# More gathers in the gates' stage, weight subtractions on GpSimd in four pieces, and w_ple's products behind the queries

## The chip, the cores and the metric

One core of a Trainium2 chip runs the whole kernel in one launch. The metric is device time in microseconds; the time of a kernel is the median of its runs. Engines are named as in the profile: PE (TensorE matmuls), PEld (its weight loads), DVE (VectorE), ACT (ScalarE), POOL (GpSimd), SP (SyncE, which here only issues DMAs).

## The reference

One layer of an encoder on 512 tokens of width 1024, in fp32. Cut to what matters here:

```python
h = rms_norm(x, norm_mix); proj = h @ w_in            # q, k, v of two attentions, two gates
merged = sigmoid(gate_na) * (out_na @ w_branch_na) + sigmoid(gate_dil) * (out_dil @ w_branch_dil)
x = x + merged @ w_out
h = rms_norm(x, norm_ffn); x = x + peer_ffn(h, ...)   # below
h = rms_norm(x, norm_ple)
x = x + sigmoid(h @ w_ple_gate) * (p @ w_ple)

# peer_ffn, 8 heads, 128 x 128 = 16384 experts of one neuron each:
q = h @ w_query                                       # per head two halves of 128
s1, s2 = q[..., :128] @ k1.T, q[..., 128:] @ k2.T
v1, i1 = top_k(s1, 16); v2, i2 = top_k(s2, 16)
sc, pos = top_k(v1[..., :, None] + v2[..., None, :], 16)
eidx = (i1 * 128 + i2) at pos;  g = softmax(sc)
a = u[eidx] . h;  act = gelu(a) * g;  out = sum act * v[eidx]
```

## The kernel before

Weights come through `Stream` W (L115 to L161): SP loads a raw block of 128 x 1024 (L130; three buffers), ACT casts it to its high half `wh` (L141), and DVE or POOL subtracts that from the raw block, which gives the low half `wl` (L142). Which of the two engines does it stands in the block's spec ("v" or "p", L122, L203). There are five pairs of halves; a product of two fp32 matrices is three matmuls, high x high, high x low and low x high (`mm3`, L163).

The experts are computed in two ways. For tokens 128 to 511 (three token blocks) the kernel is dense: it multiplies with all 128 blocks of 128 experts. `up(b)` (L1001) makes `aT` with 24 matmuls of 384 columns, ACT takes its gelu; the result is multiplied by a matrix G of gate weights; `down` (L1137) multiplies with the block's `v`, 18 matmuls of 512 columns, into six PSUM banks `outs`. For tokens 0 to 127 it gathers: `experts0` (L929) has 256 units, 128 of u and 128 of v; each is one indirect DMA on POOL of 128 rows of 4 KB into one of three buffers `gath` (L940, L941) and one DVE operation that reads it (L952 for u, L960 for v, which adds into `acc0`).

The order in the part around the change:

- merge and w_out (`xo`, L821 to L835), each token block followed by its norm (`norm_parts`, L741); behind the last of them `ple(0)` and `ple(1)` (L806, L836), p @ w_ple into a DRAM buffer, stored from ACT's queue.
- the queries (`qp`, L967) with scores and the top 16 on DVE (`top16`, L756).
- the gates' stage (L1056 to L1106): the 76 blocks "ahead" (`ahead`, L1028: `up` of blocks 0 to 75, stored to DRAM as `ge`) run beside the selection of the experts (`select_steps`, L868) and beside the building of G, 48 groups of one-hot products: DVE makes `o` (L1080) and `m` (L1085), PE multiplies them (`gp`, L1094), ACT copies them to `stage`.
- the down stage (L1154 on): per block `down`, and for the other 52 blocks also `up`; it reads `ge` and G back from DRAM. The order of fresh and stored blocks is written out in `order` (L1014 to L1024).
- the end: `done(exp_side)` (L1170), then for each of the four token blocks the third norm (`third`, L1184), whose transpositions `pt` go through PE, and the products with w_ple_gate (`pg`, L1202).

What runs "beside" is a `Side` (L41): each step of the main order reports its planned time to `tick` (L99), and each side advances by that time multiplied by its rate. For the gathers one unit costs 1.0; the rate is RATE_GATES in the gates' stage (L1058), zero while the rest of the blocks ahead is finished, RATE_HEAD for the first four blocks of the down stage, and then so set that what is left ends EARLY = 30 planned us ahead of the last block (L1157). `issue_after(latest[0])` keeps a unit behind the DVE operation marked last. The tile framework then puts each engine's queue in order, by its own simulated timeline, and sets the waits.

Of the kernel before, what the change touches and what calls it, by code (L numbers as in the profile page):

```python
# [10 lines left out]
F32 = mybir.dt.float32  # L11
# [22 lines left out]
NSP = 76  # L34

RATE_LAST, RATE_HEAD, AHEAD = 0.0, 0.1, 1.0
RATE_G, RATE_GATES, EARLY = 1.45, 0.15, 30.0
CPK = 8 + 2 + 2 + 32 + 128


# [24 lines left out]
def block_kernel(ctx: ExitStack, tc: tile.TileContext, a: dict):  # L65
    nc = tc.nc
# [14 lines left out]
    def bank(tag, name):  # L81
        return psum.tile([128, 512], F32, tag=tag, name=name, bufs=2)

    x2_d = dram.tile([3, 128, D], F32, name="x2_d")
    ple_d = dram.tile([S, D], F32, name="ple_d")
# [29 lines left out]
    class Stream:  # L115
# [17 lines left out]
        def pump(self, most=99):  # L133
            self.fetch()
            while most and len(self.cut) < len(self.raw) and len(self.cut) < self.freed + self.parts:
                i = len(self.cut)
                _, n, eng = self.specs[i]
                shape = [128, n, 1024 // n]
                hi = self.pool.tile(shape, F32R, tag=self.tag + "h", name=self.tag + "h", bufs=self.parts)
                lo = self.pool.tile(shape, F32R, tag=self.tag + "l", name=self.tag + "l", bufs=self.parts)  # L140
                nc.scalar.copy(hi, self.raw[i])  # L141
                (nc.vector if eng == "v" else nc.gpsimd).tensor_sub(lo, self.raw[i], hi.bitcast(F32))  # L142
                self.raw[i] = None
                self.cut.append((hi, lo))
                self.fetch()
                most -= 1
# [14 lines left out]
    W = Stream(wp, "w", 3, 5)  # L161

    def mm3(ps, st, mv, start, stop):  # L163
        nc.tensor.matmul(ps, st[0], mv[0], start=start, stop=False)  # L164
        nc.tensor.matmul(ps, st[0], mv[1], start=False, stop=False)  # L165
        nc.tensor.matmul(ps, st[1], mv[0], start=False, stop=stop)  # L166
# [33 lines left out]
    wpl = a["w_ple"][0].rearrange("(k p) c -> p k c", p=128)  # L200
    wpg = a["w_ple_gate"][0].rearrange("(k p) c -> p k c", p=128)

    def add_block(w, c0, width=512, lo="v"):  # L203
        n = 1024 // width
        for q in range(w.shape[1] // n):
            W.add(w[:, n * q:n * q + n, c0:c0 + width], n, lo[q % len(lo)])
# [12 lines left out]
    pT = a["pT"].rearrange("(k p) t -> p k t", p=128)  # L219
    for b in range(2):  # L220
        add_block(wo, 512 * b, lo="vp")
    for b in range(2):
        W.add(pT, 2)
        add_block(wpl, 512 * b)
    for b in range(4):
        add_block(wq, 512 * b, lo="p" if b else "vp")


    hhi = hpool.tile([128, 8, S], F32R, name="hhi")
# [71 lines left out]
    def cell(ps, st_of, units, last, mv_of=None):  # L301

        n = units[0][0].shape[1]
        nk = n * len(units)
        for u, (hi, lo) in enumerate(units):
            for k in range(n):
                kk = u * n + k
                w = (hi[:, k], lo[:, k])
                if mv_of is None:
                    mm3(ps, st_of(kk), w, kk == 0, kk == nk - 1)  # L310
                else:
                    mm3(ps, tuple(x[:, mv_of[0]] for x in w), st_of(kk), kk == 0, kk == nk - 1)
            if last:
                W.free()
            yield 3 * n * ps.shape[-1] / 2400
# [456 lines left out]
    x2p = x2s.enter_context(tc.tile_pool(name="x2p", bufs=1, side="right"))  # L772
# [6 lines left out]
    def run(gen):  # L779
        for dt in gen:  # L780
            tick(dt)

    for b in range(2):
        units = W.take(1)
        for c in range(4):
# [3 lines left out]
            ps = bank("Q", "p2")  # L789
            run(tcell(ps, units, c, (odil, odil[:, 2:4]), c == 3))  # L790
            nc.vector.tensor_mul(g, ps, g)
        units = W.take(2)
        for c in range(4):
# [4 lines left out]
            ps = bank("P", "p1")  # L798
# [4 lines left out]
            nc.vector.tensor_sub(hlo[:, cc], s, hhi[:, cc].bitcast(F32))  # L803


    def ple(b):  # L806
        (phi, plo), = W.take(1)
        units = W.take(1)
        for n in range(4):
            ps = bank("P", "pl")  # L810
            ts = slice(128 * n, 128 * n + 128)
            run(cell(ps, lambda k: (phi[:, k, ts], plo[:, k, ts]), units, False))
            po = x2p.tile([128, 512], F32, tag="po", name="po", bufs=2)
            nc.scalar.copy(po, ps)
            nc.scalar.dma_start(ple_d[128 * n:128 * n + 128, 512 * b:512 * b + 512], po)
        W.free()
        W.free()


    ss2 = x2p.tile([128, 4, 2], F32, name="ss2")  # L820
    for b in range(2):  # L821
        cols = slice(512 * b, 512 * b + 512)
        units = W.take(4)
        for n in range(4):
            ps = bank("A", "xo")
            ts = slice(128 * n, 128 * n + 128)
# [4 lines left out]
            if b:  # L831
# [1 line left out]
                    nc.scalar.dma_start(x2_d[n - 1], y)  # L833
                hn = x2p.tile([128, D], F32, tag="hn", name="hn", bufs=2) if n else h2n
                norm_parts(y, gffn, hn, ss2[:, n], ts)  # L835
    ple(0)  # L836
    ple(1)
    x2s.close()
    gts.close()
    at.close()  # L840
# [2 lines left out]
    gel = ctx.enter_context(tc.tile_pool(name="gel", bufs=1))  # L843
# [123 lines left out]
    for b in range(4):  # L967
        units = W.take(4)
        for c in range(4):
            ps = bank("A", "qp")  # L970
# [22 lines left out]
    tqs.close()  # L993


    for b in range(NB):
        W.add(a["uT"][b].rearrange("p (k e) -> p k e", k=8), 8)
    for b in range(2):
        add_block(wpg, 512 * b)

# [16 lines left out]
    k = 0  # L1017
# [41 lines left out]
    for n in range(3):  # L1059
# [13 lines left out]
        for q in range(NG):  # L1073
# [15 lines left out]
            for g in range(OG // BG):  # L1089
                gpb = bank("PC"[g % 2], "gp")  # L1090
                for x in range(BG):
                    cs = slice(128 * (BG * g + x), 128 * (BG * g + x) + 128)
# [61 lines left out]
    for i, (b, fresh) in enumerate(order):  # L1154
# [3 lines left out]
        ge = whole(b) if fresh else None  # L1158
# [7 lines left out]
    units = V.take(len(pend))  # L1166
# [29 lines left out]
    for b in range(2):  # L1196
        cols = slice(512 * b, 512 * b + 512)
        units = W.take(4)
        for n in (0, 1, 2, 3):
            ps = bank("A", "pg")  # L1200
            ts = slice(128 * n, 128 * n + 128)
            run(cell(ps, lambda k: (hhi[:, k, ts], hlo[:, k, ts]), units, n == 3))  # L1202
            pl = fin.tile([128, 512], F32, tag="pl", name="pl", bufs=2)
# [76 lines left out]
```

## Time and profile before

| | us |
|---|---|
| median of 3 runs | 1830.58 (1828.13 to 1830.72) |
| the profiled execution | 1832.46 |
| its span | 1830.7 |

| engine | busy us | share of the span |
|---|---|---|
| PE | 1776.4 | 97% |
| DVE | 1326.1 | 72% |
| ACT | 730.1 | 40% |
| POOL | 483.3 | 26% |

The span is the time from the first to the last instruction of the program in one execution; all positions below are microseconds from its start. A busy share is a mean over stages that have different limits, so the rows further down go by stage. "Idle before" an instruction is time in which its engine did nothing, and the releaser is what ended last of that for which it waited. The granted clock is a share of PE's full speed.

### The profile page before, as it was taken

The numbers are of one execution on the slowest core, as the hardware profiler recorded it, in microseconds if no ns is written. First come the engines' busy times: TensorE is split into PE (matmuls) and PEld (weight loads), VectorE is DVE, ScalarE is ACT, GpSimd is POOL, SyncE is SP. The second block draws the span as 40 slices with busy tenths as digits, with TensorE's granted clock in tenths as the row PEclk, the third lists the DMA queues.
The fourth block names the chain that finished last, engine by engine and source line by source line (L and its number), as shares of the span: only waits on it lengthen the run. The fifth ranks groups of instructions, "written<-read, shape, count | busy, mean of one in ns | idle before, by whom it ended". The sixth has DMA issues, their size and how long they took to land.

```text
span 1830.7 us, 26023 instructions
## 1 busy us (share of the span) xinstructions
PE 1776.4 (97%) x9613; PEld 1563.2 (85%) x9613; DVE 1326.1 (72%) x2642; ACT 730.1 (40%) x1195; POOL 483.3 (26%) x328
## 2 busy tenths in 40 slices
PE   8999999999999999999999999999999999999938
PEld 7997777788788999999999888888888888888827
DVE  6634644436658999988885778888888788786864
ACT  5434553442433545444444333333334233333312
POOL 4201111111233011121210334344334344343320
PEclk9999999999999999999999999999999999999969
DMA  5231123333422475777778799899999999899842
GB/s 189 74 92 45 48 55 116 90 118 124 168 97 93 148 245 174 268 289 268 277 276 315 270 358 333 320 346 360 354 326 334 362 329 341 302 345 345 305 136 81
DMA packets 158383, 417.10 MB, mean 228 GB/s; under 512 B 14000, under 2 KB 59312, under 8 KB 155184
## 3 DMA queue, kind: packets, MB, share of 16 engines
q1 hardware_dynamic: 119808, 277.54, 43.7%
q0 software_dynamic: 36864, 134.23, 20.6%
q10 hardware_dynamic: 1584, 3.67, 0.5%
q8 instruction: 75, 1.23, 0.3%
q14 instruction: 52, 0.43, 0.1%
HBM read 368.73 MB, written 45.88 MB: 226 GB/s over the span
## 4 chain that ended last, share of the span: by engine, by line
PE 54%; issue 19%; DMA 15%; POOL 5%; DVE 5%; ACT 1%; SPq 0%; POOLq 0%; DVEq 0%; ACTq 0%
PE out L1144 9%; DMA gath<-peer_expert_v,eidx 6%; POOL gath L941 5%; PE aT L165 4%; PE aT L164 4%; PE aT L166 4%; PE proj L164 3%; PE proj L165 3%; DMA gr<-ge_d 3%; PE proj L166 3%; DMA gath<-peer_expert_u,eidx 3%; DMA vr<-peer_expert_v 2%; PE gt L164 2%; PE gt L165 2%; PE gt L166 2%
## 5 line engine op out<-in xcount | busy, mean ns | idle before, releaser
L165 PE MATMUL aT<-hlo,wh 128*128 128x384 f32 x1024 | 345.1, 337 | 0.0
L166 PE MATMUL aT<-hhi,wl 128*128 128x384 f32 x1024 | 344.7, 337 | 0.0
L164 PE MATMUL aT<-hhi,wh 128*128 128x384 f32 x1024 | 344.7, 337 | 0.0
L141 ACT CAST wh<-wr 128x1024 fp32r<-128x1024 f32 x216 | 226.7, 1051 | 272.5 <-PE aT L165 214.5
L941 POOL DMA_INDIRECT gath<-peer_expert_u,eidx x128 | 191.0, 1493 | 540.0 <-DVE gath L952 376.3
L142 DVE TENSOR_TENSOR wl<-wr,wh 128x1024 fp32r<-128x1024 f32 x188 | 237.2, 1263 | 112.6 <-ACT wh L141 111.7
L941 POOL DMA_INDIRECT gath<-peer_expert_v,eidx x128 | 169.7, 1326 | 281.2 <-DVE acc L960 212.5
L1144 PE MATMUL out<-vh,ahi 128*128 128x512 f32 x768 | 235.0, 393 | 5.4 <-ACT ahi L1132 5.4
L1144 PE MATMUL out<-vl,ahi 128*128 128x512 f32 x768 | 239.3, 391 | 0.4 <-DVE vl L142 0.4
L1144 PE MATMUL out<-vh,alo 128*128 128x512 f32 x768 | 235.8, 392 | 0.0
L141 ACT CAST vh<-vr 128x1024 fp32r<-128x1024 f32 x128 | 134.2, 1050 | 158.3 <-DMA vr<-peer_expert_v 90.6
L165 PEld LDWEIGHTS aT<-hlo,wh 128*128 128x128 f32 x1024 | 192.4, 188 | 2.6
L164 PEld LDWEIGHTS aT<-hhi,wh 128*128 128x128 f32 x1024 | 192.5, 188 | 2.5
L960 DVE SCALAR_TENSOR_TENSOR acc<-gath,act,acc 128x1024 f32<-128x1024 f32 x128 | 164.2, 1283 | 40.5 <-DMA gath<-peer_expert_v,eidx 40.1
L166 PEld LDWEIGHTS aT<-hhi,wl 128*128 128x128 f32 x1024 | 192.4, 188 | 1.1
L952 DVE SCALAR_TENSOR_TENSOR gath<-gath,h2n 128x1024 f32<-128x1024 f32 x128 | 156.2, 1222 | 37.7 <-DMA gath<-peer_expert_u,eidx 37.5
L142 DVE TENSOR_TENSOR vl<-vr,vh 128x1024 fp32r<-128x1024 f32 x128 | 156.3, 1222 | 28.5 <-ACT vh L141 28.5
L1144 PEld LDWEIGHTS out<-vl,ahi 128*128 128x128 f32 x768 | 144.5, 188 | 32.2 <-DVE vl L142 0.9
L1144 PEld LDWEIGHTS out<-vh,ahi 128*128 128x128 f32 x768 | 143.4, 188 | 32.1 <-ACT ahi L1132 6.8
L1144 PEld LDWEIGHTS out<-vh,alo 128*128 128x128 f32 x768 | 144.4, 188 | 30.9 <-DVE alo L1134 0.5
L142 POOL TENSOR_TENSOR wl<-wr,wh 128x1024 fp32r<-128x1024 f32 x28 | 68.3, 2453 | 250.9 <-ACT wh L141 245.4
L164 PE MATMUL proj<-wh,hhi 128*128 128x512 f32 (+1 forms) x256 | 108.2, 425 | 7.2 <-ACT wh L141 7.2
(259 smaller groups left out, 2859.6 us busy)
## 6 DMA issues: line engine op xcount, KB each, us to landing
vr<-peer_expert_v SPq DMA_DIRECT2D x128, 512.0 KB, 6.6
wr<-uT SPq DMA_DIRECT2D x128, 512.0 KB, 4.7
g_d<-stage SPq DMA_DIRECT2D x24, 1024.0 KB, 8.7
G<-g_d SPq DMA_DIRECT2D x32, 768.0 KB, 8.5
wr<-w_in SPq DMA_DIRECT2D x46, 512.0 KB, 4.4
ge_d<-ge SPq DMA_DIRECT2D x76, 192.0 KB, 3.9
gr<-ge_d SPq DMA_DIRECT2D x76, 192.0 KB, 6.9
wr<-peer_w_query SPq DMA_DIRECT2D x16, 512.0 KB, 4.3
```

What stands on the lines that cost most here:

```text
L141: nc.scalar.copy(hi, self.raw[i])
L142: (nc.vector if eng == "v" else nc.gpsimd).tensor_sub(lo, self.raw[i], hi.bitcast(F32))
L164: nc.tensor.matmul(ps, st[0], mv[0], start=start, stop=False)
L165: nc.tensor.matmul(ps, st[0], mv[1], start=False, stop=False)
L166: nc.tensor.matmul(ps, st[1], mv[0], start=False, stop=stop)
L941: nc.gpsimd.indirect_dma_start(out=t, out_offset=None, in_=a["peer_expert_" + kind], in_offset=bass.IndirectOffsetOnAxis(ap=eidx[:, c:c + ...
L952: nc.vector.scalar_tensor_tensor(t, t, 1.0, h2n, op0=ALU.mult, op1=ALU.mult, accum_out=a0[:, c:c + 1])
L960: nc.vector.scalar_tensor_tensor(acc0, t, act0[:, c:c + 1], acc0, op0=ALU.mult, op1=ALU.add)
L1144: nc.tensor.matmul(outs[t][h], w[:, cs], x[:, h], start=first and p == 0, stop=last and p == 2)
```

## The change

Three edits. RATE_GATES goes from 0.15 to 0.37, so the planner puts more units of `experts0` into the gates' stage. The blocks of `uT` that are multiplied ahead (0 to 75), w_ple's blocks and pT are subtracted on POOL instead of DVE, and each subtraction on POOL, of these and of all other "p" blocks, becomes four of 256 columns. `ple(0)` and `ple(1)` move from ahead of the queries to behind them, with their weights behind the queries' in the stream; each product is copied and stored in two pieces of 256 columns, through the three buffers of `ge`, and the stores go to SP's queue.

```diff
-RATE_G, RATE_GATES, EARLY = 1.45, 0.15, 30.0
+RATE_G, RATE_GATES, EARLY = 1.45, 0.37, 30.0
@@ Stream.pump
-                (nc.vector if eng == "v" else nc.gpsimd).tensor_sub(lo, self.raw[i], hi.bitcast(F32))
+                if eng == "v":
+                    nc.vector.tensor_sub(lo, self.raw[i], hi.bitcast(F32))
+                else:
+                    r, h, l = (x.rearrange("p a b -> p (a b)") for x in (self.raw[i], hi, lo))
+                    for c in range(0, 1024, 256):
+                        cs = slice(c, c + 256)
+                        nc.gpsimd.tensor_sub(l[:, cs], r[:, cs], h[:, cs].bitcast(F32))
@@ order of the weight stream
-    for b in range(2):
-        W.add(pT, 2)
-        add_block(wpl, 512 * b)
     for b in range(4):
         add_block(wq, 512 * b, lo="p" if b else "vp")
+    for b in range(2):
+        W.add(pT, 2, "p")
+        add_block(wpl, 512 * b, lo="p")
@@ ple, from ahead of the queries to behind them
-            po = x2p.tile([128, 512], F32, tag="po", name="po", bufs=2)
-            nc.scalar.copy(po, ps)
-            nc.scalar.dma_start(ple_d[128 * n:128 * n + 128, 512 * b:512 * b + 512], po)
+            for c in range(0, 512, 256):
+                po = gel.tile([128, 384], F32, tag="ge", name="po", bufs=3)[:, :256]
+                nc.scalar.copy(po, ps[:, c:c + 256])
+                nc.sync.dma_start(ple_d[128 * n:128 * n + 128, 512 * b + c:512 * b + c + 256], po)
@@ weights of the up-products
-        W.add(a["uT"][b].rearrange("p (k e) -> p k e", k=8), 8)
+        W.add(a["uT"][b].rearrange("p (k e) -> p k e", k=8), 8, "p" if b < NSP else "v")
```

## Rows read from the trace of the kernel before

**Rows 1.** Busy time by stage: stretch, length, busy (instructions) per engine, PEclk, DMA share, GB/s
```profile
480.00:505.00 25.00, 23.08 (x109) 18.41 (x108) 17.80 (x32) 15.47 (x26) 3.46 (x3) 0.93 0.65 226
605.00:690.00 85.00, 85.00 (x496) 84.93 (x496) 84.27 (x391) 43.62 (x64) 8.87 (x6) 1.00 0.65 217
690.00:961.00 271.00, 271.00 (x2300) 265.17 (x2298) 244.58 (x301) 128.52 (x209) 49.31 (x24) 1.00 0.74 260
961.00:1004.00 43.00, 43.00 (x283) 42.69 (x281) 20.95 (x23) 20.48 (x31) 3.22 (x2) 1.00 0.86 313
1004.00:1743.00 739.00, 733.19 (x3476) 637.62 (x3474) 586.66 (x752) 259.66 (x357) 288.33 (x215) 1.00 0.93 333
1743.00:1774.00 31.00, 0.20 (x1) 0.00 (x0) 18.50 (x25) 2.56 (x8) 12.12 (x11) 0.56 0.54 168
1774.00:1831.00 57.00, 50.48 (x224) 41.15 (x224) 27.11 (x51) 16.39 (x28) 1.08 (x3) 0.92 0.19 65
```
**Rows 2.** Waits of PE: waiting line and releaser, us in total, times, longest
```profile
PE pt L363 <- DVE hn L750: 31.3, 1, 31.3
...
PE out L1144 <- ACT ahi L1132: 5.4, 3, 2.2
```
**Rows 3.** Timeline, end of the span: start, us, engine, line, operation, [idle before <-releaser]
```profile
1742.59 0.61 PE L1144 MATMUL out<-vh,alo 128*128 128x512 f32 x2
...
1769.11 1.28 DVE L960 SCALAR_TENSOR_TENSOR acc<-gath,act,acc 128x1024 f32<-128x1024 f32 x1 [1.23 <-DMA gath<-peer_expert_v,eidx]
...
1774.49 1.97 PE L363 MATMUL pt<-ident,hn 128*128 128x128 f32 x8 [31.29 <-DVE hn L750]
...
1824.02 0.39 PE L165 MATMUL pg<-wl,hhi 128*128 128x512 f32 x1
...
1824.47 0.39 PE L164 MATMUL pg<-wh,hhi 128*128 128x512 f32 x1
```
**Rows 4.** The gathers (line 941, POOL) by stage
```profile
690.00:961.00 271.00, 49.31 (x24) 1.00 0.74 260
...
1004.00:1743.00 739.00, 288.33 (x215) 1.00 0.93 333
```
**Rows 5.** Subtractions of weights on DVE (line 142) by stage
```profile
605.00:690.00 85.00, 25.64 (x21) 1.00 0.65 217
690.00:961.00 271.00, 61.26 (x51) 1.00 0.74 260
```
**Rows 6.** Groups of instructions: shapes, count, busy us, mean ns, idle before, releasers
```profile
L142 DVE TENSOR_TENSOR wl<-wr,wh 128x1024 fp32r<-128x1024 f32 x188 | 237.2, 1263 | 112.6 <-ACT wh L141 111.7
...
L952 DVE SCALAR_TENSOR_TENSOR gath<-gath,h2n 128x1024 f32<-128x1024 f32 x128 | 156.2, 1222 | 37.7 <-DMA gath<-peer_expert_u,eidx 37.5
...
L142 POOL TENSOR_TENSOR wl<-wr,wh 128x1024 fp32r<-128x1024 f32 x28 | 68.3, 2453 | 250.9 <-ACT wh L141 245.4 <-issue 3.4 <-PE ptp L678 1.8
...
L266 POOL TENSOR_TENSOR xsq<-xt 128x512 f32<-128x512 f32 x4 | 5.0, 1266 | 7.0 <-DMA xt<-xT 6.5 <-PE ssb L383 0.5
```
**Rows 7.** Timeline, two places where POOL and DVE subtract at the same time
```profile
461.20 2.40 POOL L142 TENSOR_TENSOR wl<-wr,wh 128x1024 fp32r<-128x1024 f32 x1 [13.68 <-ACT wh L141]
462.52 2.17 DVE L142 TENSOR_TENSOR wl<-wr,wh 128x1024 fp32r<-128x1024 f32 x1 [3.16 <-ACT wh L141]
...
497.40 2.38 POOL L142 TENSOR_TENSOR wl<-wr,wh 128x1024 fp32r<-128x1024 f32 x1 [3.43 <-issue]
...
498.73 2.14 DVE L142 TENSOR_TENSOR wl<-wr,wh 128x1024 fp32r<-128x1024 f32 x1 [2.21 <-ACT wh L141]
```
**Rows 8.** Timeline, from the last product with w_out to the first query product
```profile
486.35 0.39 PE L166 MATMUL xo<-wh,hlo 128*128 128x512 f32 x1
...
503.06 0.62 PE L164 MATMUL qp<-hhi,wh 128*128 128x512 f32 x2
```
**Rows 9.** Page, parts 3 and 6: a DMA queue (packets, MB, share of 16 engines), an issue
```profile
q0 software_dynamic: 36864, 134.23, 20.6%
...
ge_d<-ge SPq DMA_DIRECT2D x76, 192.0 KB, 3.9
```

More of the change, by code (lines that the diff above doesn't have):

```diff
@@ L803, in block_kernel @@
             nc.vector.tensor_sub(hlo[:, cc], s, hhi[:, cc].bitcast(F32))
[L806 to L812, printed above, removed]
-            po = x2p.tile([128, 512], F32, tag="po", name="po", bufs=2)
-            nc.scalar.copy(po, ps)
-            nc.scalar.dma_start(ple_d[128 * n:128 * n + 128, 512 * b:512 * b + 512], po)
-        W.free()
-        W.free()
     ss2 = x2p.tile([128, 4, 2], F32, name="ss2")
@@ L835, in block_kernel @@
                 norm_parts(y, gffn, hn, ss2[:, n], ts)
-    ple(0)
-    ple(1)
     x2s.close()
@@ L993, in block_kernel, with ple @@
     tqs.close()
+    def ple(b):
+        (phi, plo), = W.take(1)
+        units = W.take(1)
+        for n in range(4):
+            ps = bank("P", "pl")
+            ts = slice(128 * n, 128 * n + 128)
+            run(cell(ps, lambda k: (phi[:, k, ts], plo[:, k, ts]), units, False))
+            for c in range(0, 512, 256):
+                po = gel.tile([128, 384], F32, tag="ge", name="po", bufs=3)[:, :256]
+                nc.scalar.copy(po, ps[:, c:c + 256])
+                nc.sync.dma_start(ple_d[128 * n:128 * n + 128, 512 * b + c:512 * b + c + 256], po)
+        W.free()
+        W.free()
+    ple(0)
+    ple(1)
     for b in range(NB):
-        W.add(a["uT"][b].rearrange("p (k e) -> p k e", k=8), 8)
+        W.add(a["uT"][b].rearrange("p (k e) -> p k e", k=8), 8, "p" if b < NSP else "v")
     for b in range(2):
```

## The prediction

> **What bounds the kernel now.** I read the busy times by stage first, then what the matmul engine (PE) waited for, then the end of the span, and only then the prices of what moves.
>
> By stage [rows 1], PE is busy for the whole of 605 to 1004 us (the up-products of the 76 blocks ahead, beside the gates' stage) and for 733.2 of the 739 us of the down-products. Its waits are few [rows 2]: one of 31.3 us, and 5.4 us in three pieces behind the cast of `ahi`. So work taken from any other engine between 605 and 1743 shortens nothing by itself; only PE's waits can be won. The long wait lies at the end [rows 3]: the last down-product starts at 1742.6, the last gathered row is added to `acc0` at 1769.1, and only then come the norm and, at 1774.5, the first transposition. The gathers are late: 215 were issued in the 739 us of the down stage, 3.44 us each [rows 4], and the rest followed when PE was done. The granted clock, 1.00 before, falls to a mean of 0.56 over the wait and is 0.92 over the rest [rows 1]: after PE has stood idle, its first products run at the lower of its two levels, 1.2 instead of 2.4 GHz.
>
> In the gates' stage VectorE is near its limit: 84.3 of 85 us busy in 605 to 690, 244.6 of 271 in 690 to 961, together 328.9 of 356, so 27 us idle; GpSimd is busy for 49.3 of the 271 [rows 1]. VectorE is what any further gather there has to pass.
>
> **RATE_GATES from 0.15 to 0.37.** The planner's time in that stage is three selections of 18.8 (1.4 + 8 x 0.8 + 0.7 + 1.9 + 4 x 2.1) and 48 groups of 2.6, together 181. At 0.15 that makes 27 units, at 0.37 it makes 67: 40 gathers, and 40 VectorE products of 1.22 us, or 49 us [rows 6], come forward. From 1004 on 224 gathers are left now (215 and the nine after 1743); 184 will be left. At 3.44 us each they need 633 us where the stage has 739, so they end 106 us, some 31 gathers, before PE does, and the long wait goes. What is late next is the norm of the three token blocks that the down-products give, whose first blocks end four microseconds apart ahead of the last one. Without the wait the end is: last down-product at 1743, 192 gate products at 0.225 us (the spacing at full clock in rows 3; 43.2), 32 transpositions at 0.12 (eight took 1.97 at the lower clock, rows 3; 3.9), about 2 for the norm of the last block, and 6.2 from the last product to the end (1824.5 to 1830.7, rows 3): 1798.3, where it is 1830.7. That is **-32 us**; with 0 to 9 us of waiting for the norms it lies between -35 and -25.
>
> The 40 gathers also leave the DMA queues of the down stage. One takes 20.6% of 1830.7 us over 256, so 1.47 us of all 16 engines [rows 9]; 40 take 59 us. The share there falls from 0.93 to 0.85, in 690 to 961 it rises from 0.74 to 0.96. Of the 5.8 us that PE waited in the down stage I take back **-3** (0 to -6). The down stage at 0.93 cost PE no more than that, so for the gates' stage at 0.96 I add no more than 6 to its upper bound.
>
> **Subtractions to GpSimd, in four pieces.** In 605 to 961 VectorE subtracts 72 blocks in 86.9 us [rows 5]. They go; 49 us of gathers' products come: VectorE's own work falls by 38 us. A GpSimd subtraction of 1024 columns takes 2.45 us, an operation of 512 takes 1.27 [rows 6]; the line through both gives 0.67 for 256, and 2.7 for four pieces. That is 72 x 2.7 = 193 us of GpSimd's time, and with 67 gathers at 2.05 (49.3 over 24, rows 4) 330 of 399 us: it fits by itself. The pieces stand in the same queue as the gathers, and a gather waits there until VectorE has freed one of its three buffers; the pieces behind it wait too. Five pairs of halves lie between a cast and its use, some 20 us at 24 products of 0.171 us a block (496 in 85 us, rows 1), which hides that latency. The 28 blocks that GpSimd has already become 112 pieces, 28 x 0.23 = 6 us more on an engine that mostly waits there; without that cover it would cost those 6 us.
>
> The price is not GpSimd's time but VectorE's. While GpSimd subtracts, a VectorE operation that reads two tensors from SBUF stands still [rows 7]: at 462.5 such a subtraction took 2.17 us instead of the mean of 1.26 [rows 6], at 498.7 it took 2.14, and each ended 1.1 us after GpSimd's. VectorE lost 0.91 of 2.40 and 0.88 of 2.38 us, 0.38 of the operation it met, where it was busy for 17.8 of 25 us [rows 1]. At that share the 193 us cost it 73 us; scaled by how much busier it is in 605 to 961 (0.92 against 0.71), 95. Against that stand 27 us idle and 38 us of work gone, 65 together. So VectorE ends the gates' stage 8 to 30 us later, and I take **+15**, nearer the share that the rows show. The bounds are 0 (shorter pieces meet fewer operations, and PE has blocks to draw forward) and +52 (three fifths of the 193 us, less 65, and 6 for the DMA queues).
>
> No row shows GpSimd reading beside the bf16 operations of this stage, `o` and `m`. The Trainium skill (SBUF — State Buffer, Who interferes with whom) says that a VectorE instruction with two SBUF inputs contends with a GpSimd one that reads SBUF, and that the later one waits for the whole of the other; rows 7 agree for fp32, and by the page `o` and `m` would stop as well. By the page the sum is then at least the one below; were `o` and `m` left alone, it would be the second rival's.
>
> **Products with w_ple behind the queries.** Now they fill PE while the last norm is made: from the last `xo` product at 486.35 to the first query product at 503.06 are 16.7 us [rows 8], of which 48 products of 0.225 are 10.8. Without them PE waits for the norm of the last token block; its transpositions come behind the ple products now, so the queries can start 6 to 10 us earlier, and PE stands idle for about 7. The 10.8 us come back behind the queries, where PE is full. Net +1 to +5. There they use three small buffers, 16 pieces instead of 8, and their stores are on SP's queue: a store of that size lands 3.9 us after its issue [rows 9], so a piece may take 1.3 us where PE makes it in 0.7, and the loads of `uT` wait behind the stores on SP. The weights of both halves hold four of the five buffers meanwhile, so PE can draw little forward: 0 to +8. Starting the queries 8 us earlier gives VectorE's long stretch those 8 us: down to -2 in all. I take **+5** (-2 to +13).
>
> **Sum.** -32 - 3 + 15 + 5 = -15. The profiled execution took 1832.46 us, of which 1830.7 are the span; the median of the runs is 1830.58, 1.9 less. 1832.5 - 15 = 1817.5, and 1.9 less for the median: **1815.6 us**.
>
> **Rivals.**
> 1. *The port takes the place of the tail (slower).* Where VectorE is never idle, GpSimd's pieces stand between its operations one for one. If it loses 0.7 of the 193 us, that is 135, less 65 is 70, on PE, which waits for `gp`: 1832.5 - 32 - 3 + 5 + 70 - 1.9 = 1870.6. It decides from a loss of about 0.49 on (95 us, a cost of 30, where the whole change comes out even). For it: 0.92 busy, and nearly all of its work there reads two tensors. Against it: 0.38 measured, and pieces of 0.67 us, which let VectorE in four times as often. Chance 0.28, times 1834 to 1880.
> 2. *The port costs nothing.* The blocks ahead that PE has in hand cover it, as they cover a VectorE that is 92% busy now: 1832.5 - 32 - 3 + 3 - 1.9, some 1799. Chance 0.20, times 1790 to 1805.
> 3. *The change doesn't do what it says.* The gathers stick behind the pieces on GpSimd, fewer than 10 more are done by the down stage, and the tail stays for the most part; or gain and loss cancel. Times 1827 to 1834, chance 0.08.
>
> **How the numbers follow.** The forecast, 1805 to 1826, has 0.44. Faster by over 0.2% (3.7 us, about what a measurement of this kernel can tell from no change) is the forecast and the second rival, 0.64; the same 0.08; slower 0.28. All lower bounds together give 1832.5 - 35 - 6 + 0 - 2 - 1.9 = 1788, all upper ones 1832.5 - 25 + 52 + 13 - 1.9 = 1871. For 8 in 10 I cut a tenth at each side: 1793 to 1860; the likeliest sign alone would be 1793 to 1826.
>
> **What would show it.** Right: PE's wait ahead of the transpositions at the end under 5 us, no low clock there; some 67 gathers before the first down-product; VectorE's `o`, `m` and gathers' products longer in the mean than before, by some 80 us together; a new PE wait of some 7 us ahead of the queries. Wrong: PE waiting for `o` or `m`, or for `wl`, by tens of microseconds in 605 to 1004 (first rival); `o` and `m` with their old durations (second rival); under 40 gathers by the first down-product (third).

## The result, and the profile after

The changed kernel takes 1966.78 us in the median of 4 runs (1954.01 to 1972.36), the kernel before 1830.19 in 4 runs beside it: a ratio of 1.074, with a 95% interval of 1.071 to 1.077. The forecast was 1815.6 us, faster. The profiled execution of after took 1972.36 us, its span is 1970.6.

Busy time by stage of the changed kernel (columns as in [rows 1]; the stretches end where the work does, at the last gate product, the first and the last down-product):

```profile
480.00:505.00 25.00, 19.06 (x89) 15.38 (x88) 17.63 (x37) 9.83 (x16) 12.73 (x15) 0.86 0.41 148
605.00:690.00 85.00, 64.81 (x315) 59.97 (x313) 83.66 (x329) 36.32 (x63) 65.17 (x74) 0.88 0.65 202
690.00:960.00 270.00, 219.82 (x1686) 212.74 (x1686) 224.67 (x268) 93.50 (x157) 228.77 (x182) 0.90 0.65 220
960.00:1074.00 114.00, 92.37 (x729) 89.36 (x728) 80.02 (x64) 38.72 (x65) 105.29 (x80) 0.93 0.71 252
1074.00:1148.00 74.00, 65.57 (x363) 65.25 (x362) 17.46 (x16) 25.19 (x35) 33.33 (x45) 0.93 0.82 301
1148.00:1916.00 768.00, 744.91 (x3494) 641.04 (x3493) 555.74 (x722) 264.23 (x365) 249.26 (x187) 0.99 0.85 299
1916.00:1971.00 55.00, 47.77 (x224) 38.86 (x222) 26.44 (x47) 16.30 (x28) 1.09 (x2) 0.97 0.20 67
```

Set beside [rows 1] the stages add up. The first up-product starts at 605.9 us (605.0 before). From there to the first down-product are 542.5 us (399.1): **+143**. The down-products take 767.2 (738.7): **+28**. What follows takes 55.0 (87.9): **-33**. With the 0.9 that is the 139.9 us by which the span grew.

The 143 us are of two kinds. Here is the stretch from the first up-product to the first down-product as one, first of before, then of after, and ten microseconds of after:

```profile
605.00:1004.00 399.00, 399.00 (x3073) 392.79 (x3073) 349.79 (x713) 192.62 (x302) 61.41 (x32) 1.00 0.73 257
...
605.00:1148.00 543.00, 442.56 (x3088) 427.32 (x3087) 405.81 (x675) 193.72 (x318) 432.56 (x378) 0.91 0.68 235
626.00:636.00 10.00, 6.12 (x19) 6.12 (x20) 10.00 (x36) 3.73 (x6) 8.74 (x10) 0.50 0.41 132
```

PE, busy for the whole of it before, now waits for 100 us. The other 43 us are PE's own: nearly the same number of matmuls keeps it busy for 442.6 instead of 399.0 us, at a mean granted clock of 0.91 instead of 1.00. The last line shows how that comes about: from 626 to 636 us, which begins inside a wait of 6.1 us, the granted clock is 0.50, the lower of its two levels (1.2 instead of 2.4 GHz). So what makes PE wait there costs more than the wait itself.

What PE waits for from 605 to 1148 us, and then from 1148 to the end (columns as in [rows 2]; before, PE did not wait from 605 to 1004 at all):

```profile
PE gp L1103 <- DVE m L1094: 66.2, 21, 7.6
PE aT L171 <- ACT ge L1020: 29.2, 8, 8.4
...
PE out L1153 <- ACT ahi L1141: 14.5, 8, 4.1
PE out L1153 <- DVE alo L1143: 4.7, 5, 1.6
PE out L1153 <- DVE vl L143: 2.9, 6, 1.0
```

So the gates' products wait for VectorE's `m`. Why `m` is late stands in the groups of VectorE and GpSimd in the gates' stage, first of before (605 to 1004), then of after (605 to 1148); columns as in [rows 6]:

```profile
L1085 DVE TENSOR_TENSOR m<-o,iT 128x3072 bf16<-128x3072 bf16 x48 | 84.1, 1758 | 0.3
L1080 DVE TENSOR_TENSOR o<-iob,iT 128x2048 bf16<-128x2048 bf16 x48 | 58.7, 1224 | 8.6 <-PE gp L1094 8.3
L923 DVE TENSOR_TENSOR E<-E 128x512 bf16<-128x512 bf16 (+2 forms) x48 | 13.8, 321 | 0.0
...
L1094 DVE TENSOR_TENSOR m<-o,iT 128x3072 bf16<-128x3072 bf16 x48 | 99.2, 2075 | 0.3
L1089 DVE TENSOR_TENSOR o<-iob,iT 128x2048 bf16<-128x2048 bf16 x48 | 77.7, 1621 | 9.2 <-PE gp L1103 9.2
L914 DVE TENSOR_TENSOR E<-E 128x512 bf16<-128x512 bf16 (+2 forms) x48 | 28.1, 618 | 0.0
L149 POOL TENSOR_TENSOR wl<-wr,wh 128x256 fp32r<-128x256 f32 x307 | 323.1, 1086 | 27.9 <-ACT wh L141 24.1 <-issue 2.8
```

The same instructions on the same shapes take longer: `m` 0.32 us, `o` 0.40 us, the sums over `E` 0.30 us. GpSimd's pieces too: 1.09 us in the mean, 0.71 the shortest. Two places of the timeline of after show how the two engines meet:

```profile
686.21 5.52 POOL L149 TENSOR_TENSOR wl<-wr,wh 128x256 fp32r<-128x256 f32 x8
686.79 5.03 DVE L915 TENSOR_TENSOR sel<-E 128x64 f32<-128x64 bf16 x1
...
850.57 7.36 POOL L149 TENSOR_TENSOR wl<-wr,wh 128x256 fp32r<-128x256 f32 x4
851.72 1.73 DVE L1089 TENSOR_TENSOR o<-iob,iT 128x2048 bf16<-128x2048 bf16 x1
853.49 2.17 DVE L1094 TENSOR_TENSOR m<-o,iT 128x3072 bf16<-128x3072 bf16 x1
855.58 1.76 DVE L1089 TENSOR_TENSOR o<-iob,iT 128x2048 bf16<-128x2048 bf16 x1
```

At 686 us a small `sel` (0.20 us elsewhere) stands for 5.03 us beside eight pieces in a row. At 850 us they take turns: each `o` and `m` is longer by 0.4 to 0.5 us, and four pieces need 7.36 us. I call the time that VectorE's instructions are longer its **standing**: the duration of an instruction less that of the shortest tenth of its own kind (same line, names and operation) in the same run, summed over VectorE's instructions from the first up-product to the first down-product. It is 15.3 us before and 105.7 after. It is a rough measure: where two instructions overlap in VectorE and are held up together, both count.

### The profile page after: what moved, and what is told of

Read it like the earlier page. It is cut to its first block, busy times and chain, and to the rows that moved or that the text cites. A ratio compares the mean times of both kernels' runs of the same rounds, so it can differ in the third digit from the quotient of the medians.

```text
span 1970.6 us, 26470 instructions
## 1 busy us (share of the span) xinstructions
PE 1823.0 (93%) x9613; PEld 1593.6 (81%) x9613; DVE 1324.5 (67%) x2562; ACT 725.6 (37%) x1202; POOL 833.2 (42%) x732
## 4 chain that ended last, share of the span: by engine, by line
PE 56%; DVE 15%; DMA 14%; POOL 8%; issue 6%; ACT 1%; DVEq 0%; SPq 0%; POOLq 0%; ACTq 0%
PE out L1153 13%; DMA gr<-ge_d 7%; POOL wl L149 6%; DMA gath<-peer_expert_u,eidx 4%; PE aT L171 4%; PE aT L173 4%; PE aT L172 3%; PE proj L171 3%; PE proj L172 3%; PE proj L173 3%; DVE gath L943 2%; POOL gath L932 2%; DMA gath<-peer_expert_v,eidx 2%; PE gt L173 2%; PE gt L171 2%
## 5 line engine op out<-in xcount | busy, mean ns | idle before, releaser
L149 POOL TENSOR_TENSOR wl<-wr,wh 128x256 fp32r<-128x256 f32 x432 | 420.5, 1008 | 278.1 <-ACT wh L141 244.6
L171 PE MATMUL aT<-hhi,wh 128*128 128x384 f32 x1024 | 353.5, 345 | 29.2 <-ACT ge L1020 29.2
L172 PE MATMUL aT<-hlo,wh 128*128 128x384 f32 x1024 | 350.6, 342 | 0.0
L173 PE MATMUL aT<-hhi,wl 128*128 128x384 f32 x1024 | 350.5, 342 | 0.0
L1153 PE MATMUL out<-vh,ahi 128*128 128x512 f32 x768 | 238.1, 395 | 15.3 <-ACT ahi L1141 14.5
L171 PEld LDWEIGHTS aT<-hhi,wh 128*128 128x128 f32 x1024 | 198.1, 193 | 34.7 <-ACT ge L1020 31.9
L943 DVE SCALAR_TENSOR_TENSOR gath<-gath,h2n 128x1024 f32<-128x1024 f32 x128 | 167.4, 1320 | 80.2 <-DMA gath<-peer_expert_u,eidx 80.2
L143 DVE TENSOR_TENSOR wl<-wr,wh 128x1024 fp32r<-128x1024 f32 x108 | 135.6, 1257 | 113.5 <-ACT wh L141 112.7
L172 PEld LDWEIGHTS aT<-hlo,wh 128*128 128x128 f32 x1024 | 198.2, 194 | 2.9
L173 PEld LDWEIGHTS aT<-hhi,wl 128*128 128x128 f32 x1024 | 197.6, 193 | 1.0
L1153 PEld LDWEIGHTS out<-vl,ahi 128*128 128x128 f32 x768 | 144.4, 189 | 36.9 <-DVE vl L143 6.3
L185 POOL TENSOR_TENSOR r<-rv,neghalf 128x8 f32<-128x8 f32 (+1 forms) x29 | 42.0, 1452 | 249.3 <-DVE rv L184 227.0
```

Of the source, the lines that this page charges most:

```text
L143: nc.vector.tensor_sub(lo, self.raw[i], hi.bitcast(F32))
L149: nc.gpsimd.tensor_sub(l[:, cs], r[:, cs], h[:, cs].bitcast(F32))
L185: nc.gpsimd.tensor_tensor(r0, v, neghalf[:, :n], ALU.pow)
L943: nc.vector.scalar_tensor_tensor(t, t, 1.0, h2n, op0=ALU.mult, op1=ALU.mult, accum_out=a0[:, c:c + 1])
L1153: nc.tensor.matmul(outs[t][h], w[:, cs], x[:, h], start=first and p == 0, stop=last and p == 2)
```

## The experiments

All were timed in 3 rounds against the kernel before, which took 1829 to 1832 us beside them; "+" is the difference of the medians. The theory at the outset: GpSimd's subtractions beside VectorE's work make the gates' stage long. Its rivals: the added gathers do, or the moved products.

**The three parts alone, and the change without the subtractions.**

```diff
e1_rate:  before with RATE_GATES 0.15 -> 0.37
e2_subs:  before with  uT: "p" if b < NSP else "v", and "p" in four pieces
e3_ple:   before with ple(0), ple(1) behind the queries
e4_after_uT_v:  after with
-        W.add(a["uT"][b]..., 8, "p" if b < NSP else "v")
+        W.add(a["uT"][b]..., 8)
```

> The kernel before with RATE_GATES 0.37 and nothing else: 40 more gathers in the gates' stage, all subtractions where they were. Theory (the 144 us that the gates' stage of the changed kernel lasts longer come from GpSimd's subtractions beside VectorE's work): VectorE gets 49 us of products more against 27 us idle, so the first down-product starts 10 to 30 us later than at 1004, the wait at the end (31 us) goes: 1808 to 1828 us. Rival (the added gathers make the stage long, by their chain from VectorE's freeing of a buffer over GpSimd and the DMA back to VectorE): the first down-product starts near 1100 or later, 1890 to 1970 us.

> The kernel before with only the 76 blocks ahead (and the 28 blocks that GpSimd had already) subtracted by GpSimd in four pieces; RATE_GATES stays 0.15 and the products with w_ple stay in their place. Theory: VectorE loses 87 us of work and still ends later, since it stands while GpSimd's pieces run: first down-product at 1080 to 1150, the wait at the end stays: 1890 to 1960 us. Rival (added gathers): VectorE is freed of 87 us, the stage is PE-bound: first down-product at 1000 to 1010, 1825 to 1840 us.

> The kernel before with only the products with w_ple moved behind the queries, their subtractions on VectorE as before, all else as before. Theory: a wait of some 6 us before the queries, products that come back where PE is full: 1826 to 1843 us. Rival (the move itself is dear: it shares the three buffers of ge and SP's queue with the blocks ahead and delays all of them): over 1860 us.

> The changed kernel with the 76 blocks ahead subtracted by VectorE again; 0.37, the moved products and the four pieces of the 32 other blocks stay. Theory: the long stage goes, what is left are the 40 gathers (10 to 30 us) and the move (-2 to 13): 1808 to 1840 us, first down-product at 1015 to 1045. Rival (gathers or the move): most of the loss stays, over 1890 us.

Measured: e1_rate 1857.5 us (+26, ratio 1.0146, 1.0106 to 1.0187); e2_subs 1916.8 (+85; 1.0461, 1.0417 to 1.0505); e3_ple 1848.9 (+17; 1.0092, 1.0058 to 1.0127); e4_after_uT_v 1856.8 (+25; 1.0139, 1.0095 to 1.0182). The subtractions are the main part: +85 alone, 110 between e4_after_uT_v and the changed kernel. But no part is free: each of the three makes the kernel slower by itself, and e1_rate, e3_ple and e4_after_uT_v lie outside both ranges that I had given. The three parts move the first down-product from 1004 to 1044 (e1_rate), 1089 (e2_subs) and 1019 us (e3_ple): 140 us together, of the 144 that it moved in the changed kernel.

e1_rate by stretch: to the last gate product, to the first down-product, to the last one, to the end; ahead of them the second of these stretches before, behind them PE's longest wait:

```profile
969.00:1004.00 35.00, 35.00 (x210) 35.00 (x208) 15.74 (x17) 17.09 (x25) 1.01 (x1) 1.00 0.97 360
...
605.00:1021.00 416.00, 410.27 (x3121) 403.51 (x3120) 391.20 (x770) 191.06 (x301) 137.81 (x70) 0.99 0.79 279
1021.00:1044.00 23.00, 0.33 (x6) 0.15 (x3) 5.20 (x7) 3.41 (x6) 1.93 (x2) 0.56 0.95 355
1044.00:1799.00 755.00, 736.90 (x3431) 633.83 (x3432) 553.57 (x718) 262.20 (x363) 256.98 (x187) 0.99 0.86 304
1799.00:1854.00 55.00, 48.26 (x227) 39.21 (x225) 26.66 (x47) 16.30 (x28) 1.08 (x2) 0.99 0.19 67
...
PE out L1144 <- DMA gr<-ge_d: 22.8, 1, 22.8
```

The end is 55 us long, as forecast. But the last gate product comes at 1021 instead of 969 us: the 49 us of added VectorE products have moved it by 52. Before, 35 us of up-products stood behind it; here none do, so PE stands for 22.8 us until a load for the first down-product (`gr`) has landed. VectorE idles 42.6 us in this stage, 49.2 before: the idle time was hardly used at all.

In e3_ple ScalarE waits for the small buffers (first ScalarE's waits from 603 to 632 us, then two of PE's; the last is one of those before the queries):

```profile
ACT po L989 <- DMA ple_d<-po: 7.1, 3, 3.9
...
PE aT L164 <- ACT ge L1013: 6.6, 1, 6.6
PE pt L363 <- DVE hlo L754: 5.1, 2, 4.7
```

Its profiled execution was a long one (1855.4 us); there the down-products take 748.5 us, 10 more than before.

**What of the subtractions costs.** Three kernels change e2_subs in the one line of GpSimd's pieces, or in what PE reads:

```diff
e7_subs_memset
-    nc.gpsimd.tensor_sub(l[:, cs], r[:, cs], h[:, cs].bitcast(F32))
+    nc.gpsimd.memset(l[:, cs].bitcast(F32), 0.0)
e10_subs_memset_long
+    nc.gpsimd.memset(l.bitcast(F32), 0.0)
e9_subs_unread: in up(b)
-    mm3(ps, (hi[:, k], lo[:, k]), ...)
+    mm3(ps, (hi[:, k], (hi if b < NSP else lo)[:, k]), ...)
```

> The kernel with the subtractions alone (+86 us), in which GpSimd's four pieces write zeros instead of subtracting: same count, same place in its queue, no reading. It leaves out the low halves of those weights. Theory (VectorE stands while GpSimd reads SBUF): VectorE's o, m and gathers' products fall back to their durations of before and the loss goes: 1825 to 1850 us. Rival (GpSimd's queue itself, the waits between cast, piece and product, is what costs): most of it stays, over 1880 us.

> The kernel with the subtractions alone (+86 us), in which the third product of each block ahead reads the high half of the weights instead of the low one, so PE never waits for GpSimd; GpSimd subtracts as before. The low halves of these blocks are left out of the result. Theory (VectorE's standing is the cause, PE waits for m and for the gates): nearly all stays, 1890 to 1925 us. Rival (PE and the casts wait for GpSimd's late low halves): most of the loss goes, under 1860 us.

> As the kernel that writes zeros instead of subtracting, but each of the four pieces writes all 1024 columns, so that GpSimd is busy about as long as with subtractions (a piece took 0.32 us at 256 columns; 1 us or so is wanted) without reading SBUF. The low halves are left out of the result. Theory (reading beside VectorE is the cause): still no loss, 1822 to 1850 us. Rival (GpSimd's long queue and the weights buffers that it holds are the cause, and the short writes hid that): 1880 to 1920 us.

Measured: e7_subs_memset 1829.4 us (ratio 1.000, 0.998 to 1.002): the whole loss is gone. e9_subs_unread 1922.8 (1.0506, 1.0471 to 1.0540): all of it stays, though PE waits for no low half; so GpSimd's being late is not the cause. e10_subs_memset_long 1861.2 (+30; 1.0153, 1.0086 to 1.0219) lies between what the theory and what the rival gave: a third of the loss is back. VectorE's and GpSimd's groups in it, then a place of its timeline:

```profile
L1092 DVE TENSOR_TENSOR m<-o,iT 128x3072 bf16<-128x3072 bf16 x48 | 84.1, 1755 | 0.7
L1087 DVE TENSOR_TENSOR o<-iob,iT 128x2048 bf16<-128x2048 bf16 x48 | 58.6, 1221 | 44.7 <-PE gp L1101 44.6
L149 POOL MEMSET wl<- 128x1024 f32 x300 | 281.5, 959 | 61.2 <-PE aT L173 42.0 <-PE qp L173 10.9
...
619.61 15.29 POOL L149 MEMSET wl<- 128x1024 f32 x17
621.01 13.97 DVE L1051 CAST iob<-iotaf 128x128 bf16<-128x128 f32 x1
```

GpSimd is about as busy as with the subtractions (281.5 us of writes), and `o` and `m` have their old durations: what only writes does not stop them. It stops others, which read one tensor: the cast to `iob` stood for 13.97 us beside 17 writes in a row, and the shift and the mask of the positions took 3.7 us in the mean, mostly in one place where both stood for 11.5 us at the same time. All of that lies in the selections of the experts: PE is busy for 68.4 of the 85 us from 605 to 690, and for 267.1 of the next 270, where the gates' products are (in e2_subs for 72.4 and 230.8).

This is what the Trainium skill states (SBUF — State Buffer, Who interferes with whom): a VectorE instruction with two SBUF inputs contends with a GpSimd one that reads SBUF and not with one that only writes it, while casts and `tensor_scalar` can take both ports and contend with either. Rows of after, 2.075 us for `m` and 1.621 for `o`, and of e10_subs_memset_long, 1.755 and 1.221, agree.

The writes also take away something else: they read neither the raw block nor its cast, so the raw block comes free earlier and SP can load the next one. ScalarE's waits for the loads of `uT`, from 605 to 1090 us, are 2.2 us before, 21.7 in e2_subs and 2.8 in e10_subs_memset_long. e8_subs_whole, below, tells how much that is worth: there these waits are 4.1 us, and 75 of the 85 us are lost all the same. So it is not the main part.

**How the loss grows.**

```diff
e12_subs_half:  e2_subs with  "p" if b < NSP and b % 2 else "v"
e8_subs_whole:  e2_subs with one tensor_sub of 1024 columns for "p"
e15_both: before, in which "v" subtracts the blocks ahead as before, and besides
+    for c in range(0, 1024, 256):
+        nc.gpsimd.tensor_sub(self.spare, r[:, cs], h[:, cs].bitcast(F32))
e11_subs_ahead:  e2_subs with AHEAD 1.0 -> 1.6
```

> The kernel with the subtractions alone (+86 us), but only every second of the 76 blocks ahead is subtracted by GpSimd, the others by VectorE as before. Theory (each piece beside VectorE's work costs about the same): half of the loss, 1865 to 1885 us. Rival (the first half is paid from the 43 us that VectorE is relieved of and from the blocks that PE has in hand): 1822 to 1845 us.

> The kernel with the subtractions alone (+86 us), each as one GpSimd instruction of 1024 columns. Theory (a VectorE operation waits for the GpSimd instruction that runs, and with pieces back to back for those behind it too): GpSimd's busy time is some 176 instead of 194 us and the loss is the same or up to 30 us smaller: 1885 to 1925 us. Rival (shorter pieces let VectorE in more often): whole ones are dearer by more than 10 us, 1930 to 1990 us.

> The kernel before, in which VectorE subtracts the 76 blocks ahead as before and GpSimd subtracts them too, in four pieces each, into a spare tile that nobody reads; all else as before. It differs from the kernel with the subtractions alone (1917 us) in that VectorE is relieved of nothing. Theory (what VectorE is relieved of pays for nothing as long as PE sets the stage's end, and what it stands still reaches PE one for one): 1910 to 1945 us, no more than 30 above. Rival (the relief of 87 us pays in full, and the stalls are dearer by as much): 1975 to 2010 us.

> The kernel with the subtractions alone (+86 us) with AHEAD 1.6 instead of 1.0: more up-products stand between the gates' products in PE's queue and fewer behind the last of them. Theory (VectorE's stalls reach PE because its queue has the gates' products where a VectorE that never stands would have them ready, and the up-products that could cover them stand 81 us behind the last gate): the up-products cover part of the stalls, 1850 to 1895 us. Rival (PE's order matters little; the stall itself is the loss): 1905 to 1925 us.

Measured: e12_subs_half 1874.6 us (1.0239, 1.0187 to 1.0290), e8_subs_whole 1904.0 (1.0399, 1.0369 to 1.0429), e15_both 1952.2 (1.0665, 1.0623 to 1.0707), e11_subs_ahead 1909.0 (1.0441, 1.0384 to 1.0497). Here they are beside each other with VectorE's standing (as defined above) and its busy time from the first up-product to the first down-product:

| kernel | time against before, us | VectorE busy, us | standing, us | last gate product | first down-product |
|---|---|---|---|---|---|
| before | 0 | 350 | 15 | 969 | 1004 |
| e7, short writes | 0 | 266 | 11 | 922 | 1002 |
| e10, long writes | +30 | 293 | 52 | 953 | 1032 |
| e12, half of the blocks | +44 | 351 | 54 | 989 | 1042 |
| e8, whole | +75 | 365 | 109 | 996 | 1074 |
| e11, up-products earlier | +78 | 345 | 86 | 1065 | 1087 |
| e2, all in pieces | +85 | 347 | 89 | 1008 | 1089 |
| e15, VectorE subtracts too | +121 | 464 | 123 | 1088 | 1126 |

Two things are to be read here. First, the time follows the standing, 0.8 to 1.2 us for each us above the 15 of before, and half of the blocks cost half: nothing covers a first part of it. (In e10 the measure is off: the shift and the mask that stood together count twice, and the cast, the only one of its kind, not at all. Each counted once, its standing is some 29 us above that of before, for +30.) Second, what VectorE is relieved of is worth little. In e7_subs_memset its busy time falls by 84 us, and the kernel is not a microsecond faster; in e15_both it carries 73 subtractions more (89 us at 1.22 each) than in e2_subs, and the time grows by 36. The 34 us by which its standing is longer (its own subtractions stand too) are enough for that:

```profile
L142 DVE TENSOR_TENSOR wl<-wr,wh 128x1024 fp32r<-128x1024 f32 x80 | 117.4, 1469 | 39.0 <-ACT wh L141 39.0
```

(the group of e15_both in that stage; 1.22 us each without pieces beside them). e15_both came out 7 us above the theory's bound and 23 under the rival's. That none of the 36 us is the missing relief is argued from the sizes and not shown: ScalarE's waits for the loads of `uT` rise as well, from 21.7 to 76.8 us.

Where the relief goes shows in the last gate product. Stretches of e7_subs_memset, then of e2_subs, each to the last gate product and from there to the first down-product:

```profile
603.00:922.00 319.00, 316.87 (x2594) 310.73 (x2593) 252.08 (x613) 157.98 (x257) 120.86 (x268) 1.00 0.74 254
922.00:1002.00 80.00, 80.00 (x468) 79.96 (x466) 13.91 (x14) 31.98 (x45) 12.87 (x48) 1.00 0.74 262
...
605.00:1008.00 403.00, 340.94 (x2606) 328.82 (x2605) 333.30 (x614) 157.47 (x257) 325.72 (x275) 0.93 0.57 200
1008.00:1089.00 81.00, 79.67 (x463) 79.35 (x461) 13.44 (x13) 31.71 (x44) 36.66 (x53) 1.00 0.77 276
```

The gates are drawn forward: nearly the same number of matmuls stands ahead of the last gate product in both (2594 and 2606), and some 465 behind it, where there were 35 us of them before. In e2_subs the gates then come 86 us later than in e7_subs_memset, PE waits in the order of its queue, and the 81 us of up-products behind them cover nothing. Of the 85 us that e2_subs loses by the first down-product 63 are waits of PE (484 less 340.9 and 79.7), and some 21 are PE's longer work, at a granted clock of 0.93 in the mean up to the last gate product. e11_subs_ahead tested whether that place is the cause: only 21 us of up-products were left behind the last gate, and the loss was 78 us all the same. So it is not the order alone, and my theory of the order fell. In e2_subs VectorE idles 137 us of the stage, 38.9 of them waiting for PE's `gp` and 26.3 for gathers, while ScalarE waits 35.6 us for `E` of VectorE with the `ge` that PE needs in the same queue: the engines wait for each other in turn. That this ring is why no idle time takes up the standing is argued from these waits; no run isolates it.

Whole instructions (e8_subs_whole) cost some 10 us less than pieces, at the edge of what the two intervals tell apart: four times as many openings did not help.

**Pieces held apart.** Could gaps between the pieces let VectorE in?

```diff
e16_subs_gaps: e2_subs, behind each piece of a block ahead
+    nc.gpsimd.memset(self.spare, 0.0)
e17_subs_gaps2: the same between two pieces, bound to its place
+    with tc.issue_after(last):
+        last = nc.gpsimd.memset(self.spare, 0.0).ins
+    with tc.issue_after(last):
+        last = nc.gpsimd.tensor_sub(l[:, cs], r[:, cs], h[:, cs].bitcast(F32)).ins
```

> The kernel with the subtractions alone (1917 us), with a write of 128x256 zeros (0.32 us, reads nothing) behind each piece of the blocks ahead, into a spare tile. Theory (GpSimd keeps VectorE out from one piece to the next, and a gap of 0.32 us lets it in): VectorE's short operations no longer take 3 to 5 us, the loss falls by 15 to 40 us, 1875 to 1905 us. Rival (each piece costs VectorE its own time, whatever stands between, and GpSimd is only busier): 1915 to 1950 us.

> The kernel with the subtractions alone (1917 us), in which the four pieces of a block ahead are held apart by a write of 128x256 zeros (0.31 us, reads nothing) between each two, in that order. Theory (GpSimd keeps VectorE out from one piece to the next, and 0.31 us without reading lets it in): the stalls of 3 to 6 us on VectorE's short operations go, and the loss falls by 10 to 40 us, 1877 to 1907 us. Rival (each piece that meets an operation costs its 0.7 us, with or without a gap, and the rare long stalls are a small part): 1910 to 1935 us.

e16_subs_gaps, 1921.9 us (1.0481, 1.0430 to 1.0531), is inconclusive: the planner put the writes elsewhere, and eight pieces still ran in a row at 735 us. In e17_subs_gaps2, 1932.1 us (1.0568, 1.0539 to 1.0597), they stand where they should, and the long stalls are there as before (its timeline):

```profile
741.67 7.81 DVE L940 TENSOR_TENSOR E<-E 128x256 bf16<-128x256 bf16 x4
...
742.55 0.72 POOL L154 TENSOR_TENSOR wl<-wr,wh 128x256 fp32r<-128x256 f32 x1
743.23 0.30 POOL L152 MEMSET spare<- 128x256 f32 x1
743.50 0.73 POOL L154 TENSOR_TENSOR wl<-wr,wh 128x256 fp32r<-128x256 f32 x1
```

GpSimd runs on at its undisturbed 0.72 us while VectorE's sums over `E` stand. The rival was right: gaps of that kind open nothing, and GpSimd's added 0.3 us make it a little worse.

**The moved products with four small buffers.**

```diff
e13_ple_ge4: e3_ple with  tag="ge", bufs=3 -> 4  (po and ge)
```

> The kernel with the products with w_ple moved and nothing else (+17 us), with four of the small buffers that these products share with ge instead of three. Theory (the casts of these products wait for a buffer whose store has not landed, and the first ge of the blocks ahead stands behind them: 7.1 us of waits and a gap of 6.8 us on PE): 5 to 9 us less, 1838 to 1844 us. Rival (the move costs by the waits before the queries and by SP's queue): 1846 to 1852 us as before.

1846.7 us (1.0088, 1.0061 to 1.0114), not to be told from e3_ple's 1848.9 and in the rival's range. PE's wait for `ge` fell from 6.6 to 4.0 us; the waits before the queries (4.7 and 3.8 us) stayed. The buffers are a part, and a fourth one does not take it away.

**Fewer gathers.**

```diff
e6_rate25:  before with RATE_GATES 0.15 -> 0.25
e14_rate20: before with RATE_GATES 0.15 -> 0.20
```

> The kernel before with RATE_GATES 0.25 and nothing else: about 18 more gathers in the gates' stage instead of 40. Theory (VectorE bounds the gates' stage, and each added product moves its end one for one, but 35 us of up-products behind the last gate cover the first of that): 18 x 1.22 = 22 us are covered, first down-product at 1004 to 1012, some 206 gathers left at 3.44 us = 709 us of the 739, so the wait at the end goes: 1798 to 1812 us. Rival (the down stage is what suffers from gathers that come earlier, or the price is linear in the gathers): 18 of 40 of the measured +26 us, 1835 to 1848 us.

> The kernel before with RATE_GATES 0.20 and nothing else, some 9 more gathers in the gates' stage. Theory (the up-products behind the last gate cover the first 20 us or so of added VectorE work, and each gather brought forward takes 3.4 us off the wait at the end): 9 x 1.22 = 11 us are covered, 9 x 3.4 = 31 us of the wait go: 1798 to 1812 us, under the kernel with 0.25 (1816). Rival (0.25 is the better place, the wait at the end is not gone with 0.20): 1817 to 1828 us.

e6_rate25 took 1816.2 us (ratio 0.9925, 0.9899 to 0.9951), e14_rate20 1816.6 (0.9939, 0.9910 to 0.9967): both faster than the kernel before, by 13 to 15 us. Both lie 4 us above the theory's range, and 0.20 is no better than 0.25. e6_rate25 from the first to the last down-product, and from there to the end:

```profile
1019.00:1757.00 738.00, 727.85 (x3432) 629.96 (x3432) 578.61 (x752) 259.59 (x364) 295.20 (x208) 1.00 0.91 328
1757.00:1812.00 55.00, 48.66 (x226) 39.14 (x224) 27.85 (x54) 16.16 (x30) 1.63 (x3) 0.97 0.19 67
```

It wins the 33 us at the end, as the change did, and pays 15 us in the gates' stage (first down-product at 1019); its down-products take 738 us as before. At 0.20 the first down-product comes at 1012 and 11.3 us of the wait at the end are left (in a profiled execution of 1823.1 us, 6.5 above the median). So the first part of the change was worth having at a quarter to half of its size: 9 or 17 gathers brought forward instead of 39.

## Why the prediction was wrong

- **PE bounds the kernel, only its waits can be won.** Right, and more right than I made use of: e7_subs_memset takes 84 us from VectorE and wins nothing. What it leaves out is that PE's own work is longer at the lower clock behind its waits; the sum counts that cost at the end of the span alone, and in the gates' stage it was 43 us.
- **The wait at the end, -32 us.** Right: the stretch behind the last down-product went from 87.9 to 55.0 us, -33; 71 gathers were issued before the first down-product, 39 more than before (40 forecast).
- **The down stage, -3.** Wrong: +28. The DMA share fell as forecast, from 0.93 to 0.85, but PE's waits there rose from 5.8 [rows 1] to 22.9 us, and PE is busy for 744.9 instead of 733.2. VectorE's waits for the loads of `gr` rose from 30.3 to 72.3 us. e1_rate has +16 there (and 72.7 us of these waits), e6_rate25 with 0.25 none (36.9). So 16 of the 28 us come with the large rate, and not from slower transfers: a load of `gr` landed after 6.9 us in the median before and after 6.7 in e1_rate. Why VectorE then meets them too early was not found, and the other 12 us have no run of their own.
- **Added VectorE products, 49 us into 27 us of idle time.** This failed. e1_rate moved the last gate by 52 us. What covers such a shift is not VectorE's idle time but the up-products behind the last gate, 35 us of them; once they are used up, PE waits for a load, 22.8 us that the prediction did not see.
- **GpSimd's price, 193 us for 72 blocks.** Nearly right: 0.71 us for the shortest of 307 pieces, where the line through [rows 6] gave 0.67; busy 323 us with its own waits.
- **VectorE's loss, 73 to 95 us.** Right: 105.7 of standing less 15.3 is 90 in the changed kernel, some 74 in e2_subs. The share of 0.38 from two fp32 meetings [rows 7] held for the whole stage with its bf16 operations: 90 is 0.41 of 307 pieces at 0.71 us, 74 is 0.35 of e2_subs' 296.
- **65 us of slack against it.** This is the step that failed. I subtracted 27 idle and 38 relieved microseconds of VectorE from its loss, as if PE followed VectorE's total. PE follows the dates of `m` and `ge`: relief pulls the gates forward and pays nothing (e7_subs_memset), standing pushes them back and costs in full. With the slack left out the forecast's own numbers give a cost of 73 to 95 for +15 (1874 to 1896 us); the first rival's 135 us, without its 65, gives 1935. The slack was taken away in both, which is most of why even the rival's upper end, 1880, lay 87 us low. It does not close the sum: 1896 is still 71 us short. 31 of these are the down stage. The others lie in the gates' stage, where two things stood at nothing: the 49 us of gathers' products, set off against subtractions whose leaving paid nothing, and PE's lower clock. How much each has in the 143 us no run separates.
- **Products with w_ple, +5 (-2 to +13).** The places were right, the size not: +17 alone in e3_ple. The waits before the queries came as forecast (3.5 and 2.4 us in after), the small buffers held ScalarE for 7.1 us and PE for 6.6, and PE ran at the lower clock behind each gap. Beside the large rate the move costs nothing (e4_after_uT_v and e1_rate are equal), which fits a VectorE that is late there anyway, but no run shows that as the reason.
- **28 blocks in pieces, nothing.** Agrees as far as it was tested: e4_after_uT_v has these pieces and is no slower than e1_rate.
- **Two bounds are added up wrongly.** Three fifths of the 193 us, less 65, and 6 are +57, not +52; and 0 to 9 us of waiting behind -32 give -32 to -23, not -35 to -25. Neither would have brought the measured time into the range.

So the sign followed the first rival: the port took the place of the tail. The chance of 0.28 for it rested on an offset that the prediction's own first step spoke against: where PE is full and only its waits can be won, the 38 us of work gone from VectorE shorten nothing by themselves. What was to show that rival, PE waiting for `m` by tens of microseconds, is there (66.2 us); its price is not: VectorE lost 90 us, not 135.

## What to carry to other kernels

An engine's idle time in a stage is not a purse: ask where in its queue it lies, and what the bounding engine has left behind the last result that it takes from it. An operation that is moved to GpSimd to relieve VectorE costs what VectorE then stands still. In this kernel that counted in full, since PE waits for VectorE's results in the order of its queue and then works at a lower clock, while the relief was worth nothing as long as PE was full. When one change holds three edits, time each alone, and the useful one at half its size: here that was worth 13 us.

## What was not expected of the hardware

At some places VectorE does not get in between two instructions of GpSimd: a `sel` of 0.20 us stood 5.03 us beside eight pieces, a cast 13.97 us beside 17 writes, and four sums over `E` took 7.81 us although writes of 0.3 us, which stop no such sum by themselves (in e7_subs_memset none took over 0.42 us), stood between the pieces. At other places (850 us) the two engines take turns, piece for operation. Which of the two happens was not settled; these long stalls are few (four above 1.5 us in after, of 172 above 0.2 us), and most of the standing is made of the short ones.
